# One encoder block on one core: each engine's instructions in the program's own order

## The chip, the cores and the metric

The kernel runs on one core of a Trainium2 chip. TensorE (PE) multiplies matrices and transposes, VectorE (DVE) and ScalarE (ACT) work elementwise, GpSimd (POOL) takes a little, SyncE (SP) issues the transfers. The time is that of one execution on the device in microseconds (us). The kernel before takes 1742.75 us, the median of three runs (1742.09 to 1745.59).

## The reference

256 tokens of 2048 channels, float32. What is computed, cut to its steps:

```python
mod = silu(c) @ w_cond + b_cond                  # six vectors: shift, scale, gate, twice
u = x * (1 + sc_m) + sh_m
cb, cc, ch, q, k, v, qi, ki, wi, ga, gb = split(u @ w_in)
y_a = cb * causal_dwconv3(cc * ch)               # short convolution
y_b = sparse_attention(q, k, v, qi, layer_norm(ki), wi)   # top 64 keys by an indexer's score
merged = sigmoid(ga) * (y_a @ w_a) + sigmoid(gb) * (y_b @ w_b)
x = layer_norm(ALPHA * x + (1 + g_m) * (merged @ w_o))    # the first norm
u = x * (1 + sc_f) + sh_f
a, b = split(u @ w_up)                           # 2 x 5632 channels
x = layer_norm(ALPHA * x + (1 + g_f) * ((gelu(causal_dwconv3(a)) * b) @ w_down))
```

## The kernel before

Every weight arrives as a *unit* of 1 MB (128 x 2048 float32), loaded by SP into one of four buffers `raw`. A unit is split for TensorE into an upper part, `hi` (ACT, line 82, a rounding copy), and the rest, `lo` (DVE, line 84, raw minus hi). There are three buffers of each. The activations are split in the same way, and a product is made of hi·hi, lo·hi and hi·lo. The function `unit` does load, hi and lo; a unit is multiplied by `xstat` (activations stationary, 24 matmuls of 512 columns), `wstat` (weights stationary, 16 matmuls of 512 columns and 16 of 256) or, in the segments, `seg_blocks`/`seg_tokens` (48 of 256 or 24 of 512).

The stages, in order: segments 0 to 3 of the input projection, beside which the 32 products of `c` with `w_cond` for the first shift and scale are made (`cond`, line 183: 1 MB and one DVE pass each, called a *dot* below) and u is made from them block by block (`modulated`); the index key `kw`; segment 4 with the indexer and the first two head groups of the attention; segments 5 and 6 with the other two and the convolution; 16 units `cb` of `w_in`; the gates and outputs (`columns`), each in units of `xstat`; `w_o` and the first norm; the first 24 of the 44 channel blocks of `w_up` and their part of `w_down`, then the other 20 and theirs; the second norm. A channel block takes two units, here slot *a* (product `ha`) and slot *g* (product `hg`). After slot a come: copy of one half of the product (ACT, line 119), sum (DVE, line 120), convolution (ACT line 333, DVE line 335 twice), gelu (ACT, line 653); after slot g: copy, sum, product (line 658), and the split of the result (ACT line 88, DVE line 89). Another 64 dots are spread over the stages by a running credit (`background`).

The order on every engine's queue is set by a scheduler, which goes by its own timing model. Where the program says `tc.issue_after`, an instruction stands behind another: that is so around the first norm (the last units of `w_o`, the first of `w_up`). The normalised rows are scaled and shifted by GpSimd (lines 618, 619) right behind that norm, while the first channel blocks run.

Of the kernel before, what the change touches and what calls it, by code (L numbers as in the profile page):

```python
# [41 lines left out]


C_B, C_C, C_H, C_Q, C_K, C_V, C_QI, C_KI, C_GA, C_GB = (
    0, 2048, 4096, 6144, 8192, 8704, 9216, 10240, 10320, 12368)


@with_exitstack
def hybrid_block(ctx: ExitStack, tc: tile.TileContext, t, out):
# [23 lines left out]
    def raw(src, width=D):  # L73
        r = wts.tile([P, D], F32, tag="raw", bufs=4, name="raw")
        nc.sync.dma_start(r[:, :width], src)
        return r

    def unit(src, width=D):

        r = raw(src, width)  # L80
# [28 lines left out]
    def wstat(pss, ws, x, m=P):  # L109

        for k in range(KB):
            for ps, (hi, lo) in zip(pss, ws):
                wh, wl = hi[:, k * m:(k + 1) * m], lo[:, k * m:(k + 1) * m]
                nc.tensor.matmul(ps, wh, x.both(k), start=k == 0, stop=k == KB - 1, skip_group_check=True)  # L114
                nc.tensor.matmul(ps[:, :S], wl, x.parts(k)[0], start=False, stop=k == KB - 1, skip_group_check=True)  # L115
# [6 lines left out]
    def xstat(ps, ws, x, b0, first, last, done=None):  # L122

        def tokens(n, units):
            s = slice(n * P, (n + 1) * P)
            for j in units:
                hi, lo = ws[j]  # L130
                for i in range(G4):
                    xh, xl = x.parts(b0 + j * G4 + i)
                    wh, wl = hi[:, i * 512:(i + 1) * 512], lo[:, i * 512:(i + 1) * 512]
                    a = first and j == 0 and i == 0
                    z = last and j == len(ws) - 1 and i == G4 - 1
                    nc.tensor.matmul(ps[n], xh[:, s], wh, start=a, stop=False)  # L136
                    nc.tensor.matmul(ps[n], xh[:, s], wl, start=False, stop=False)  # L137
                    end = nc.tensor.matmul(ps[n], xl[:, s], wh, start=False, stop=z)  # L138
            return end

        every = range(len(ws))
        end = tokens(0, every)
        if done:
            mid = done(0) or end
            with tc.issue_after(end.ins):
                tokens(1, every[:-1])
            with tc.issue_after(mid.ins):
                tokens(1, every[-1:])
            done(1)
        else:  # L150
            tokens(1, every)

    def groups(n, last):

        return [(g, 1) for g in range(n)] if not last else [(g, 1) for g in range(n - 3)] + [(n - 3, 3)]
# [9 lines left out]


# [6 lines left out]
    row_of(c_col, [c_b[:, g * 512:(g + 1) * 512] for g in range(4)])  # L173
    bcond = const.tile([P, 6, KB], F32)
    nc.sync.dma_start(bcond, t["b_cond"])
    mhalf = const.tile([P, 1], F32)
    nc.vector.memset(mhalf, -0.5)
    mod = const.tile([P, 6, KB], F32)


    def cond(p, k):
        r = raw(t["w_cond"][p * KB + k])
        nc.vector.scalar_tensor_tensor(  # L183
            r, r, 1.0, c_b, op0=ALU.mult, op1=ALU.mult, accum_out=mod[:, p, k:k + 1])
        one = 0.0 if p in (0, 3) else 1.0
        nc.vector.tensor_scalar(
            mod[:, p, k:k + 1], mod[:, p, k:k + 1], bcond[:, p, k:k + 1], one,
            op0=ALU.add, op1=ALU.add)

    later = [(p, k) for p in (2, 3, 4, 5) for k in range(KB)]  # L190
    credit = [0.0]

    def background(rate):
        credit[0] += rate
        while credit[0] >= 1.0 and later:
            credit[0] -= 1.0
            cond(*later.pop(0))
# [4 lines left out]

    def modulated(k):
        g, i = divmod(k, G4)
        cond(0, k)
        cond(1, k)
        if i == 0:
            xt[g] = act(f"xt{g}")
            nc.sync.dma_start(xt[g], t["x_t"][g])
        x, (hi, lo) = xt[g][:, i, :], u.parts(k)  # L210
        nc.scalar.activation(x, x, AF.Identity, scale=mod[:, 1, k:k + 1], bias=mod[:, 0, k:k + 1])
        nc.scalar.copy(hi, x)  # L212
        nc.gpsimd.tensor_sub(lo, x, hi.bitcast(F32))  # L213

    def proj(c0, name):
        ps = bank(name)
        wstat([ps], [unit(t["w_in"][c0])], u)
        return ps
# [4 lines left out]
    vt = acts.tile([P, NT, 512], F32, tag="act", bufs=25, name="v")  # L223
    cc, ch = [[acts.tile([P, NT, 512], F32, tag="act", bufs=25, name=f"{x}{g}") for g in range(4)] for x in ("cc", "ch")]
# [3 lines left out]

    def flat(x):
        return x.rearrange("p a b -> p (a b)")  # L230
# [21 lines left out]

    done = [0]

    def ahead(k):

        while done[0] < k:
            modulated(done[0])
            done[0] += 1
# [27 lines left out]
    def segment(sg, to, each=None, lead=0):  # L287

        k0, k1, u0, u1, n = SEGS[sg]
        num = (u1 - u0) * 512 // n  # L290
        start = max(done[0], k1)
        if lead:
            ws, pss = [], [[bank("s") for _ in range(n // 256)] for _ in range(lead)]
            for k in range(k0, k1):
                ahead(k + 1)
                if k - k0 < lead:
                    ws.append(unit(t[f"w_s{sg}"][k - k0], (k1 - k0) * n))
                for j in range(len(ws)):
                    for kk in range(k0 if j == k - k0 else k, k + 1):
                        for c in range(n // P):  # L300
                            seg_blocks(pss[j][c // 2][:, c % 2 * S:(c % 2 + 1) * S], ws[j], kk, kk - k0, n, c,
                                       kk == k0 and c % 2 == 0, kk == k1 - 1)
        ahead(k1)
        for j in range(num):
            if j < lead:
                ps = pss[j]
            else:
                w = unit(t[f"w_s{sg}"][j], (k1 - k0) * n)
                ps = [bank("s") for _ in range(n // 256)]
                seg_unit(sg, j, w, ps)  # L310
            seg_end(sg, j, ps)
# [4 lines left out]
    segment(0, 4, lead=2)  # L316
    segment(1, 5)
    segment(2, 8)

    conv_a = const.tile([P, KB, 3], F32)  # L320
    nc.sync.dma_start(conv_a, t["conv_a"])
    conv_f = const.tile([P, NFF, 3], F32)
    nc.sync.dma_start(conv_f, t["conv_f"])
    ln1 = const.tile([P, 2, KB], F32)
    nc.sync.dma_start(ln1, t["ln1_cols"])
    idx_gb = const.tile([P, 2, 2], F32)
    nc.vector.memset(idx_gb, 0.0)
    for j in range(2):
        nc.sync.dma_start(idx_gb[64 * j:64 * j + 64, j, :], t["idx_gb"])
# [17 lines left out]
    def indexer():  # L347

        zz = tmp.tile([P, 2, P], F32, tag="t1k", bufs=4, name="zz")
# [25 lines left out]

        for n in range(NT):
# [3 lines left out]
            for h0 in range(0, IH, per):  # L380
# [8 lines left out]
                for i in range(per):  # L389
# [377 lines left out]
```

## Time and profile before

| | |
|---|---|
| median of three runs | 1742.75 us |
| profiled execution | 1740.17 us, of it the span 1738.4 us |
| PE busy | 1691.0 us (97%), mean granted clock 0.989 |
| DVE busy | 1235.8 us (71%) |
| ACT busy | 759.3 us (44%) |
| POOL busy | 81.6 us (5%) |
| transfers | 419.58 MB, 241 GB/s over the span |

A share of the span is an average over stages, so the stages are looked at one by one. In a timeline a row gives the start, the duration, engine, line and operation; what stands in brackets is how long the engine was idle before, and who ended that. PE's ends are modelled, so a matmul's price is best taken as the distance between starts, or as stretches divided by their matmuls.

### The profile page before, as it was taken

To read this page: it belongs to the slowest core of one execution; us is meant where nothing else is said; L and a number is where in the kernel's file an instruction comes from. 1 tells how busy PE (TensorE), PEld (TensorE's weight loads), DVE (VectorE), ACT (ScalarE), POOL (GpSimd) and SP (SyncE) were. 2 spreads that over 40 slices of the span, in tenths; PEclk is the share of its full clock that TensorE was granted. 3 is DMA by queue.
4 is the path that set the end of the run, shared out by engine and by line. 5 is a ranking of instruction groups with operands and counts; after the bars stand their busy time and mean duration, and the time that the engine had idled before them with its cause. 6 is when DMAs were issued, how large, how long until landed. Compare 5 with 4: busy or idle time off the path is not lost.

```text
span 1738.4 us, 21791 instructions
## 1 busy us (share of the span) xinstructions
PE 1691.0 (97%) x8942; PEld 1451.3 (83%) x8942; DVE 1235.8 (71%) x1350; ACT 759.3 (44%) x824; POOL 81.6 (5%) x56
## 2 busy tenths in 40 slices
PE   6998999999999999999999799999999999999997
PEld 6888799988888888888888688888888888888885
DVE  6888968988888666776777797666654466666555
ACT  5553334444545333433333545544433344454431
POOL 1011100000000000000000530000000000000002
PEclk8999999999999999999999999999999999999999
DMA  8998865677786777777787476555555555555651
GB/s 329 342 363 345 334 244 202 238 258 269 272 309 242 273 288 267 265 280 272 266 302 282 143 290 218 194 186 185 187 192 194 193 194 184 181 193 188 233 194 64
DMA packets 63268, 419.58 MB, mean 241 GB/s; under 512 B 7616, under 2 KB 7744, under 8 KB 14528
## 3 DMA queue, kind: packets, MB, share of 16 engines
q1 hardware_dynamic: 63168, 418.18, 66.1%
q8 instruction: 70, 1.15, 0.2%
q14 instruction: 30, 0.25, 0.0%
HBM read 416.06 MB, written 2.10 MB: 241 GB/s over the span
## 4 chain that ended last, share of the span: by engine, by line
PE 89%; DVE 6%; DMA 2%; issue 1%; ACT 1%; POOL 0%; POOLq 0%; DVEq 0%; ACTq 0%
PE ha L114 9%; PE hg L114 9%; PE m L137 5%; PE m L136 5%; PE m L138 5%; PE ha L115 5%; PE hg L115 5%; PE y L138 5%; PE y L137 5%; PE y L136 5%; PE g L137 3%; PE g L136 3%; PE g L138 3%; PE s L250 3%; PE s L251 3%; PE s L249 3%
## 5 line engine op out<-in xcount | busy, mean ns | idle before, releaser
L84 DVE TENSOR_TENSOR lo<-raw,hi 128x2048 fp32r<-128x2048 f32 (+2 forms) x301 | 675.9, 2247 | 385.0 <-ACT hi L82 384.2
L82 ACT CAST hi<-raw 128x2048 fp32r<-128x2048 f32 (+2 forms) x301 | 561.0, 1864 | 662.5 <-PE m L138 150.0
L114 PE MATMUL ha<-u,hi 128*128 128x512 f32 x704 | 250.7, 397 | 0.0
L114 PE MATMUL hg<-u,hi 128*128 128x512 f32 x704 | 248.9, 395 | 0.0
L183 DVE SCALAR_TENSOR_TENSOR raw<-raw,c_b 128x2048 f32<-128x2048 f32 x96 | 223.1, 2328 | 35.8 <-DMA raw<-in_w_cond 29.4
L115 PE MATMUL ha<-u,lo 128*128 128x256 f32 x704 | 198.2, 281 | 4.3 <-DVE lo L84 4.3
L115 PE MATMUL hg<-u,lo 128*128 128x256 f32 x704 | 197.3, 280 | 0.0
L114 PEld LDWEIGHTS ha<-u,hi 128*128 128x128 f32 x704 | 132.7, 189 | 31.0 <-issue 0.2
L114 PEld LDWEIGHTS hg<-u,hi 128*128 128x128 f32 x704 | 131.9, 187 | 30.8
L237 PE MATMUL s<-u,hi 128*128 128x256 f32 x448 | 129.9, 293 | 9.7 <-ACT u L212 7.3
L115 PEld LDWEIGHTS ha<-u,lo 128*128 128x128 f32 x704 | 133.8, 190 | 4.7 <-DVE lo L84 4.6
L136 PE MATMUL y<-hi,h 128*128 128x512 f32 x352 | 137.0, 389 | 0.0
L137 PE MATMUL y<-lo,h 128*128 128x512 f32 x352 | 136.9, 389 | 0.0
L138 PE MATMUL y<-hi,h 128*128 128x512 f32 x352 | 136.9, 389 | 0.0
L115 PEld LDWEIGHTS hg<-u,lo 128*128 128x128 f32 x704 | 133.0, 189 | 0.0
L239 PE MATMUL s<-u,lo 128*128 128x256 f32 x448 | 127.6, 290 | 3.8 <-DVE lo L84 3.7
L238 PE MATMUL s<-u,hi 128*128 128x256 f32 x448 | 128.8, 289 | 0.7 <-POOL u L213 0.7
L250 PE MATMUL s<-lo,u 128*128 128x512 f32 (+1 forms) x304 | 116.1, 382 | 3.6 <-DVE lo L84 3.5
L251 PE MATMUL s<-hi,u 128*128 128x512 f32 (+1 forms) x304 | 116.5, 383 | 0.0
L249 PE MATMUL s<-hi,u 128*128 128x512 f32 (+1 forms) x304 | 113.6, 381 | 1.4 <-ACT hi L82 1.4
L137 PE MATMUL g<-lo,u 128*128 128x512 f32 x256 | 99.9, 390 | 0.0
L138 PE MATMUL g<-hi,u 128*128 128x512 f32 x256 | 99.8, 390 | 0.0
(172 smaller groups left out, 2643.9 us busy)
## 6 DMA issues: line engine op xcount, KB each, us to landing
raw<-in_w_cond SPq DMA_DIRECT2D x96, 1024.0 KB, 5.3
raw<-in_w_up SPq DMA_DIRECT2D x88, 1024.0 KB, 4.8
raw<-in_w_s SPq DMA_DIRECT2D x56, 1024.0 KB, 5.0
raw<-in_w_down SPq DMA_DIRECT2D x44, 1024.0 KB, 4.8
raw<-in_w_g SPq DMA_DIRECT2D x32, 1024.0 KB, 4.9
raw<-in_w_in SPq DMA_DIRECT2D x16, 1024.0 KB, 4.9
raw<-in_w_a SPq DMA_DIRECT2D x16, 1024.0 KB, 4.9
raw<-in_w_b SPq DMA_DIRECT2D x16, 1024.0 KB, 5.1
```

Of the source, the lines that this page charges most:

```text
L82: nc.scalar.copy(hi[:, :width], r[:, :width])
L84: nc.vector.tensor_sub(lo[:, :width], r[:, :width], hi[:, :width].bitcast(F32))
L114: nc.tensor.matmul(ps, wh, x.both(k), start=k == 0, stop=k == KB - 1, skip_group_check=True)
L115: nc.tensor.matmul(ps[:, :S], wl, x.parts(k)[0], start=False, stop=k == KB - 1, skip_group_check=True)
L136: nc.tensor.matmul(ps[n], xh[:, s], wh, start=a, stop=False)
L137: nc.tensor.matmul(ps[n], xh[:, s], wl, start=False, stop=False)
L138: end = nc.tensor.matmul(ps[n], xl[:, s], wh, start=False, stop=z)
L183: nc.vector.scalar_tensor_tensor(r, r, 1.0, c_b, op0=ALU.mult, op1=ALU.mult, accum_out=mod[:, p, k:k + 1])
L237: nc.tensor.matmul(ps, hi[:, a], xh, start=first, stop=False, skip_group_check=True)
L249: nc.tensor.matmul(ps[m], xh[:, s], hi[:, a], start=first and k == k0, stop=False)
L250: nc.tensor.matmul(ps[m], xh[:, s], lo[:, a], start=False, stop=False)
L251: nc.tensor.matmul(ps[m], xl[:, s], hi[:, a], start=False, stop=last and k == k1 - 1)
```

## The change

Everything is issued under `tc.manual_schedule()`: each engine's queue has the order in which the program emits. The program first writes a list, `stream`, of steps (one per unit), loads and single calls, and a loop at the end emits it. For each step s it emits `parts` of the step three further on (`AHEAD`), then one piece each of two queues of side work (attention, convolution), then at some steps a dot, then the products of s, then what follows s. There are four buffers of hi and of lo instead of three. The attention, the indexer and the convolution are generators that give way after each piece. The first norm is written out as `first_norm` and `first_norm2`: the token-0 half of the last `w_o` units goes first, rows are normalised by DVE and ACT, transposes are issued a group at a time, and the weights of the blocks behind it may not be split before it ends (`hold`). The rows' scale and shift on GpSimd come at channel blocks 6, 9, 12 and 15. Before the first product TensorE makes 40 transposes of the identity, and 20 more behind the first one (`keep_warm`). The second norm runs on DVE alone, and its last product is finished in halves of 256 columns.

```diff
+AHEAD = 3
+LOADS = 4
...
-        hi = wts.tile([P, D], F32R, tag="hi", bufs=3, name="hi")
-        nc.scalar.copy(hi[:, :width], r[:, :width])
-        lo = wts.tile([P, D], F32R, tag="lo", bufs=3, name="lo")
-        nc.vector.tensor_sub(lo[:, :width], r[:, :width], hi[:, :width].bitcast(F32))
-        return hi, lo
+        hi = wts.tile([P, D], F32R, tag="hi", bufs=4, name="hi")
+        nc.scalar.copy(hi[:, :n], r[:, :n])
...
+        lo = wts.tile([P, D], F32R, tag="lo", bufs=4, name="lo")
+        nc.vector.tensor_sub(lo[:, :n], r[:, :n], hi[:, :n].bitcast(F32))
...
+        def after_a():
+            x = t1k("ha")
+            total(x, pa[0])
+            y.append(t1k("hy"))
+            conv3(y[0], x, conv_f[:, f, :])
+            nc.scalar.activation(y[0], y[0], AF.Gelu_apprx_tanh)
...
+            if half == 0 and f in (6, 9, 12, 15):
+                do(ln_apply, (f - 6) // 3)
...
+    for s in stream:
...
+        at += 1
+        while prepared < min(at + AHEAD, len(steps)):
+            x = steps[prepared]
+            if x.hold and x.hold not in passed:
+                break
+            if not x.by_hand:
+                order.append(parts(x))
+            prepared += 1
+        order.append(lambda: [piece(x) for x in queues])
+        if later:
+            credit += s.cond
+            if credit >= 1.0:
+                credit -= 1.0
+                order.append(later_dot())
+        if s.mm:
+            order.append(lambda s=s: s.mm(s.w))
+        if s.after:
+            order.append(s.after)
...
+    with tc.manual_schedule():
```

ScalarE in the channel blocks of `w_up`, before (`hi` the split of a coming unit, `ha` and `b` the copies of a product's half, `hy` the convolution, line 333, and the gelu, line 653, `h` the split result):

```order
L82 CAST hi_8581<-raw_8579 128x2048
L119 COPY b_8478<-hg_8393 128x256
L653 ACTIVATE hy_8435<-hy_8435 128x256
L88 CAST h08_8482<-hy_8435 128x256
L82 CAST hi_8627<-raw_8625 128x2048
L119 COPY ha_8525<-ha_8485 128x256
L333 ACTIVATE hy_8528<-ha_8525,conv_f_1014 128x256
L82 CAST hi_8674<-raw_8672 128x2048
L119 COPY b_8571<-hg_8486 128x256
L653 ACTIVATE hy_8528<-hy_8528 128x256
L82 CAST hi_8720<-raw_8718 128x2048
```

The same engine and place now (line 120 is the split, 167 the copy, 422 the convolution, 880 the gelu, 136 the split result):

```order
L120 CAST hi_7857<-raw_7719 128x2048
L167 COPY b_7897<-hg_7864 128x256
L136 CAST h02_7901<-hy_7850 128x256
L120 CAST hi_7906<-raw_7808 128x2048
L167 COPY ha_7943<-ha_7910 128x256
L422 ACTIVATE hy_7946<-ha_7943,conv_f_85 128x256
L880 ACTIVATE hy_7946<-hy_7946 128x256
L120 CAST hi_7953<-raw_7855 128x2048
L167 COPY b_7990<-hg_7957 128x256
L136 CAST h02_7901<-hy_7946 128x256
L120 CAST hi_7998<-raw_7861 128x2048
```

Before, a split of a coming unit stood between the convolution and the gelu of a block; now gelu stands directly behind the convolution, and the next split behind the gelu.

VectorE there, before (`lo` the split of a coming unit, `ha` and `b` the sums, `hy` twice line 335 and once the product, `h` the split result):

```order
L84 TENSOR_TENSOR lo_8583<-raw_8579,hi_8581 128x2048
L120 TENSOR_TENSOR b_8478<-b_8478,hg_8393 128x256
L658 TENSOR_TENSOR hy_8435<-hy_8435,b_8478 128x256
L89 TENSOR_TENSOR h08_8482<-hy_8435,h08_8482 128x256
L84 TENSOR_TENSOR lo_8629<-raw_8625,hi_8627 128x2048
L120 TENSOR_TENSOR ha_8525<-ha_8525,ha_8485 128x256
L335 SCALAR_TENSOR_TENSOR hy_8528<-ha_8525,conv_f_1014,hy_8528 128x255
L335 SCALAR_TENSOR_TENSOR hy_8528<-ha_8525,conv_f_1014,hy_8528 128x254
```

And now (line 126 is `lo`, 244 a dot, 168 the sums, 424 the convolution):

```order
L126 TENSOR_TENSOR lo_7717<-raw_7614,hi_7715 128x2048
L244 SCALAR_TENSOR_TENSOR raw_7620,mod_82<-raw_7620,c_b_78 128x2048
L168 TENSOR_TENSOR ha_7755<-ha_7755,ha_7722 128x256
L424 SCALAR_TENSOR_TENSOR hy_7758<-ha_7755,conv_f_85,hy_7758 128x255
L424 SCALAR_TENSOR_TENSOR hy_7758<-ha_7755,conv_f_85,hy_7758 128x254
L126 TENSOR_TENSOR lo_7767<-raw_7667,hi_7765 128x2048
L168 TENSOR_TENSOR b_7802<-b_7802,hg_7769 128x256
L898 TENSOR_TENSOR hy_7758<-hy_7758,b_7802 128x256
L137 TENSOR_TENSOR h00_7710<-hy_7758,h00_7710 128x256
```

The rows of this engine keep their sequence; the dot now has a fixed place between a `lo` and the sum behind it, and the `lo` of a row belongs to the unit three further on.

VectorE in segment 3, before (`lo` line 84, dots line 183, what is added to a dot line 186, sums of the segment's products line 285):

```order
L84 TENSOR_TENSOR lo_1456<-raw_1452,hi_1454 128x2048
L84 TENSOR_TENSOR lo_1514<-raw_1510,hi_1512 128x2048
L183 SCALAR_TENSOR_TENSOR raw_1544,mod_107<-raw_1544,c_b_78 128x2048
L285 TENSOR_TENSOR q3_114<-q3_114,s_1458 128x512
L183 SCALAR_TENSOR_TENSOR raw_1548,mod_107<-raw_1548,c_b_78 128x2048
L186 TENSOR_SCALAR mod_107<-mod_107,bcond_103 128x1
L285 TENSOR_TENSOR q3_114<-q3_114,s_1459 128x512
L186 TENSOR_SCALAR mod_107<-mod_107,bcond_103 128x1
L84 TENSOR_TENSOR lo_1562<-raw_1558,hi_1560 128x2048
```

And now (`lo` line 126, sums line 354, dots line 244, line 289 the addition behind two dots):

```order
L126 TENSOR_TENSOR lo_1545<-raw_1473,hi_1543 128x2048
L354 TENSOR_TENSOR q3_95<-q3_95,s_1547 128x512
L354 TENSOR_TENSOR q3_95<-q3_95,s_1548 128x512
L126 TENSOR_TENSOR lo_1603<-raw_1531,hi_1601 128x2048
L354 TENSOR_TENSOR cc0_97<-cc0_97,s_1605 128x512
L354 TENSOR_TENSOR cc0_97<-cc0_97,s_1606 128x512
L244 SCALAR_TENSOR_TENSOR raw_1534,mod_82<-raw_1534,c_b_78 128x2048
L244 SCALAR_TENSOR_TENSOR raw_1541,mod_82<-raw_1541,c_b_78 128x2048
L289 TENSOR_TENSOR mod_82<-mod_82,bcond_79 128x2
L126 TENSOR_TENSOR lo_1650<-raw_1599,hi_1648 128x2048
```

Before, both sums of a unit could stand behind the dots and the `lo` ahead of them; now the dots stand behind both sums of the second unit, and the next `lo` behind the addition to the dots. On ScalarE two instructions that make u from that addition stand ahead of the next split:

```order
L120 CAST hi_1543<-raw_1473 128x2048
L120 CAST hi_1601<-raw_1531 128x2048
L290 ACTIVATE u12_1641<-xt3_1633,mod_82 128x256
L295 ACTIVATE xt3_1633<-xt3_1633,mod_82 128x256
L120 CAST hi_1648<-raw_1599 128x2048
L120 CAST hi_1682<-raw_1635 128x2048
```

So the split of the unit after next is behind those two, and they are behind the dots.

## Rows read from the trace of the kernel before

**Rows 1.** Windows: start:end, length, busy of PE, PEld, DVE, ACT, POOL, clock, DMA share, GB/s.

```profile
0.00:220.00 220.00, 198.03 (x1151) 174.46 (x1152) 186.27 (x190) 101.55 (x113) 29.99 (x22) 0.95 0.91 343
220.00:960.00 740.00, 739.35 (x3822) 630.78 (x3821) 565.48 (x647) 311.12 (x319) 1.11 (x2) 1.00 0.72 266
960.00:1040.00 80.00, 67.40 (x364) 57.35 (x363) 68.92 (x86) 41.05 (x61) 39.69 (x24) 0.94 0.61 212
```

**Rows 2.** Windows of two stretches of 40 us: columns, and channel blocks.

```profile
640.00:680.00 40.00, 40.00 (x178) 33.11 (x178) 24.43 (x18) 15.77 (x9) 0.00 (x0) 1.00 0.74 282
1080.00:1120.00 40.00, 40.00 (x232) 35.26 (x231) 26.12 (x30) 19.57 (x25) 0.00 (x0) 1.00 0.52 184
```

**Rows 3.** Timeline of ACT in a channel block of w_up.

```profile
1132.16 0.41 ACT L88 CAST h<-hy 128x256 fp32r<-128x256 f32 x1 [2.64 <-DVE hy L658]
1132.57 1.91 ACT L82 CAST hi<-raw 128x2048 fp32r<-128x2048 f32 x1
...
1137.17 0.51 ACT L333 ACTIVATE hy<-ha,conv_f 128x256 f32<-128x256 f32 x1 [2.43 <-DVE ha L120]
...
1140.19 0.42 ACT L653 ACTIVATE hy<-hy 128x256 f32<-128x256 f32 x1
```

**Rows 4.** Timeline of DVE in the same block.

```profile
1131.18 0.42 DVE L120 TENSOR_TENSOR b<-b,hg 128x256 f32<-128x256 f32 x1
1131.70 0.43 DVE L658 TENSOR_TENSOR hy<-hy,b 128x256 f32<-128x256 f32 x1
...
1134.51 2.29 DVE L84 TENSOR_TENSOR lo<-raw,hi 128x2048 fp32r<-128x2048 f32 x1 [1.49 <-ACT hi L82]
1136.72 0.42 DVE L120 TENSOR_TENSOR ha<-ha 128x256 f32<-128x256 f32 x1
1137.71 1.01 DVE L335 SCALAR_TENSOR_TENSOR hy<-ha,conv_f,hy 128x255 f32<-128x255 f32 x2 [0.58 <-ACT hy L333]
```

**Rows 5.** Timeline: first norm on DVE, PE, POOL, and w_down's first matmul.

```profile
963.78 0.69 DVE L595 TENSOR_TENSOR v<-gm,m 128x512 f32<-128x512 f32 x1 [3.92 <-PE m L138]
...
982.64 3.61 PE L566 MATMUL zT<-ident,v 128*128 128x128 f32 x16 [8.20 <-ACT v L562]
...
996.09 3.38 DVE L183 SCALAR_TENSOR_TENSOR raw<-raw,c_b 128x2048 f32<-128x2048 f32 x1
...
1000.56 16.07 POOL L619 TENSOR_TENSOR v<-v,lnrow 128x512 f32<-128x512 f32 x6
...
1260.42 0.48 PE L136 MATMUL y<-hi,h 128*128 128x512 f32 x1
```

**Rows 6.** Timeline of PE: start of segment 3, last matmul of kw.

```profile
116.49 0.28 PE L237 MATMUL s<-u,hi 128*128 128x256 f32 x1
...
220.16 0.28 PE L115 MATMUL kw<-u,lo 128*80 128x256 f32 x1
```

**Rows 7.** Timeline of DVE and ACT in segment 3.

```profile
139.09 2.29 DVE L183 SCALAR_TENSOR_TENSOR raw<-raw,c_b 128x2048 f32<-128x2048 f32 x1
141.29 0.69 DVE L285 TENSOR_TENSOR v<-v,s 128x512 f32<-128x512 f32 x1
...
145.07 0.60 ACT L211 ACTIVATE xt<-xt,mod 128x256 f32<-128x256 f32 x1 [1.25 <-DVE mod L186]
145.70 0.41 ACT L212 CAST u<-xt 128x256 fp32r<-128x256 f32 x1
```

**Rows 8.** Groups by form: side work of attention and convolution.

```profile
L420 DVE SCALAR_TENSOR_TENSOR lg<-lg,sc 128x512 f32<-128x512 f32 x12 | 8.0, 684 | 1.5 <-PE lg L417 1.5
L424 DVE TENSOR_REDUCE mx<-lg 128x4 f32<-128x1024 f32 x4 | 4.9, 1218 | 0.0
L431 DVE TENSOR_SCALAR lg<-lg,sm 128x128 f32<-128x128 f32 x16 | 3.5, 281 | 0.0
...
L427 ACT ACTIVATE lg<-lg,mx 128x256 f32<-128x256 f32 x16 | 7.9, 498 | 0.1
```

**Rows 9.** Timeline of the tail: POOL's last instruction.

```profile
1733.44 1.59 POOL L629 TENSOR_TENSOR v<-v,ln 128x512 f32<-128x512 f32 x1
```

More of the change, by code (lines that the diff above doesn't have):

```diff
@@ L120, in total, with xstat @@
         nc.vector.tensor_add(dst, dst, ps[:, :S])
[L122 to L155, printed above, removed]
+    def xstat(ps, w, x, b0, n, first=False, last=False, cols=512):
+        s = slice(n * P, (n + 1) * P)
+        hi, lo = w
+        for c in range(0, 512, cols):
+            y = ps[:, c:c + cols]
+            for i in range(G4):
+                xh, xl = x.parts(b0 + i)
+                o = i * 512 + c
+                wh, wl = hi[:, o:o + cols], lo[:, o:o + cols]
+                a, z = first and i == 0, last and i == G4 - 1
+                nc.tensor.matmul(y, xh[:, s], wh, start=a, stop=False, skip_group_check=True)
+                nc.tensor.matmul(y, xh[:, s], wl, start=False, stop=False, skip_group_check=True)
+                nc.tensor.matmul(y, xl[:, s], wh, start=False, stop=z, skip_group_check=True)
     def row_of(cols, dst):
@@ L164, in row_of, with flat, beside, piece @@
             nc.scalar.copy(dst[g], ps)
+    def flat(x):
+        return x.rearrange("p a b -> p (a b)")
+    queues = {"attend": [], "conv": []}
+    def beside(queue, work, *a):
+        do(lambda: queues[queue].append(work(*a)))
+    def piece(queue):
+        while queues[queue]:
+            try:
+                next(queues[queue][0])
+                return
+            except StopIteration:
+                queues[queue].pop(0)
+    def drain(queue):
+        while queues[queue]:
+            piece(queue)
     c_col = const.tile([P, KB], F32)
@@ L193, in background, with keep_warm @@
[L193 to L197, printed above, removed]
+    half_sums = const.tile([P, 2, 2], F32)
+    conv_a = const.tile([P, KB, 3], F32)
+    conv_f = const.tile([P, NFF, 3], F32)
+    ln1 = const.tile([P, 2, KB], F32)
+    idx_gb = const.tile([P, 2, 2], F32)
+    nc.vector.memset(idx_gb, 0.0)
+    def keep_warm(n):
+        ps = abank("warm")
+        for _ in range(n):
+            nc.tensor.transpose(ps[:, :P], ident, ident)
@@ new lines, in dot, with use @@
+    def dot(p, k, halves=False):
+        def use(r):
+            for h in range(2 if halves else 1):
+                a = slice(h * 1024, (h + 1) * 1024) if halves else slice(0, D)
+                nc.vector.scalar_tensor_tensor(
+                    r[:, a], r[:, a], 1.0, c_b[:, a], op0=ALU.mult, op1=ALU.mult,
+                    accum_out=half_sums[:, p, h:h + 1] if halves else mod[:, p, k:k + 1])
+            if p > 1 and k == KB - 1:
+                nc.vector.tensor_add(mod[:, p], mod[:, p], bcond[:, p])
+        return Load(t["w_cond"][p * KB + k], -D if halves else D, use)
@@ L210, in modulated @@
[L210 to L218, printed above, removed]
+        if k == 0:
+            stream.extend([dot(0, 0, True), dot(1, 0, True)])
+        else:
+            if i == 0:
+                do(xload, g)
+            stream.extend([dot(0, k), dot(1, k)])
@@ L285, in seg_end, with ahead, segment, mm @@
                 nc.vector.tensor_add(y, y, p)
-    def segment(sg, to, each=None, lead=0):
+    made = [0]
+    def ahead(k):
+        while made[0] < k:
+            modulated(made[0])
+            made[0] += 1
+    def segment(sg, to, first=0, each=None, cond=0.0):
         k0, k1, u0, u1, n = SEGS[sg]
         num = (u1 - u0) * 512 // n
[L291 to L302, printed above, removed]
-        ahead(k1)
[L304 to L309, printed above, removed]
+        start = max(made[0], k1)
+        ahead(k1)
+        for j in range(first, num):
+            ps = []
+            def mm(w, j=j, ps=ps):
+                ps += [bank("s") for _ in range(n // 256)]
                 seg_unit(sg, j, w, ps)
-            seg_end(sg, j, ps)
+            step(t[f"w_s{sg}"][j], mm, lambda j=j, ps=ps: seg_end(sg, j, ps), (k1 - k0) * n, cond)
             ahead(start + min(to - start, (to - start) * (j + 2) // num))
@@ L428, in attend, with weights @@
                                      accum_out=sm[:, i:i + 1])
+            return lg, sm
+        def weights(lg, sm):
             nc.vector.reciprocal(sm, sm)
@@ L498, in columns @@
+        step(t["w_in"][j], mm, after, cond=0.3)
+    do(drain, "conv")
+    do(drain, "attend")
     def columns(name, w, c, x, each):
[L500 removed]
+        ps = []
         for g in range(4):
[L502 to L512 removed]
@@ L514, in hybrid_block, with mm, gated, gate_row @@
-    ma = [gated(c, ya, 0, "w_a") for c in range(4)]
+            def mm(w, g=g):
+                if g == 0:
+                    ps.extend([bank(name), bank(name)])
+                for n in range(NT):
+                    xstat(ps[n], w, x, g * G4, n, g == 0, g == 3)
+            step(t[w][c * 4 + g], mm, (lambda: [each(n, ps[n]) for n in range(NT)]) if g == 3 else None, cond=0.6)
+    def gated(c, x, gate, w, m):
+        sg = []
+        def gate_row(n, ps):
+            if n == 0:
+                sg.append(rows_tile("sg"))
+                m.append(rows_tile("ma"))
+            nc.scalar.activation(sg[0][:, n, :], ps, AF.Sigmoid)
+        columns("g", "w_g", gate * 4 + c, u, gate_row)
+        columns("m", w, c, x, lambda n, ps: nc.vector.tensor_mul(m[-1][:, n, :], ps, sg[0][:, n, :]))
@@ L560, in modulated2, with gains, normed @@
+    def gains():
+        nc.vector.tensor_mul(ab[:, 0, :], ln1[:, 0, :], mod[:, 4, :])
+        nc.vector.tensor_mul(ab[:, 1, :], ln1[:, 1, :], mod[:, 4, :])
+        nc.vector.tensor_add(ab[:, 1, :], ab[:, 1, :], mod[:, 3, :])
+    do(gains)
+    po = pm
+    ends = [step(t["w_o"][12 + g]) for g in (1, 2, 3)]
+    def normed(n, rs, off, on_act):
         for g in range(KB // G4):
             y = v[g][:, n, :]
-            nc.scalar.activation(y, y, AF.Identity, scale=rs, bias=off)
-            ps = abank("zT")
@@ new lines, in parts2, with first_norm @@
+    def parts2(n, g, x, h, eng):
+        w = u2.pair(g * G4 + 2 * h)
+        hi, lo = w[:, :, 0, n * P:(n + 1) * P], w[:, :, 1, n * P:(n + 1) * P]
+        nc.scalar.copy(hi, x[:, 2 * h:2 * h + 2, :])
+        eng.tensor_sub(lo, x[:, 2 * h:2 * h + 2, :], hi.bitcast(F32))
+    up1 = Step(t["w_up"][NFF], None, None, D, 0.0, None, True)
+    def first_norm():
+        ws = [s.w for s in ends]
+        for n in (0,):
+            for i, w in enumerate(ws):
+                xstat(po[n], w, mg, (i + 1) * G4, n, False, i == 2)
+        gated_rows(3, 0, po[0])
+        mean, rs = moments(st, 0)
+        off0 = offset(mean, rs)
+        normed(0, rs, off0, ())
+        for i in (0, 1):
+            xstat(po[1], ws[i], mg, (i + 1) * G4, 1)
@@ L652, in hybrid_block @@
-            conv3(y, x, conv_f[:, f, :])
-            nc.scalar.activation(y, y, AF.Gelu_apprx_tanh)
-            if f > 0:
-                wstat([pg], [unit(t["w_up"][NFF + f])], u2)
-            b = t1k("b")
-            total(b, pg)
-            nc.vector.tensor_mul(y, y, b)
-            split(*h.parts(f - f0), y)
-            with tc.issue_after(ends[1][1].ins):
-                background(0.75)
-        if half == 0:
-            while later:
-                cond(*later.pop(0))
-            gf = tmp.tile([P, D], F32, tag="row", name="gf")
-            gf = [gf[:, g * 512:(g + 1) * 512] for g in range(4)]
-            row_of(mod[:, 5, :], gf)
@@ L691, in hybrid_block, with mm @@
-            for g, m in groups(ng, final):
-                ws = [unit(t["w_down"][c * (NFF // G4) + f0 // G4 + g + i]) for i in range(m)]
-                xstat(pm, ws, h, g * G4, g == 0, g + m == ng, done if m > 1 else None)
-            if not final:
-                done(0)
-                done(1)
+            for g in range(ng - 3 if final else ng):
+                def mm(w, g=g, pm=pm, h=h, ng=ng):
+                    if g == 0:
+                        pm += [bank("y0"), bank("y1")]
+                    for n in range(NT):
+                        xstat(pm[n], w, h, g * G4, n, g == 0, g == ng - 1)
+                step(t["w_down"][c * (NFF // G4) + f0 // G4 + g], mm,
+                     (lambda c=c, pm=pm, half=half: [down_rows(c, n, pm[n], half) for n in range(NT)])
+                     if g == ng - 1 else None)
@@ new lines, in hybrid_block, with finish @@
+            if final:
+                last = [step(t["w_down"][c * (NFF // G4) + f0 // G4 + g]) for g in range(ng - 3, ng)]
+                def finish(pm=pm, h=h, ng=ng):
+                    for n in range(NT):
+                        for i, s in enumerate(last):
+                            xstat(pm[n], s.w, h, (ng - 3 + i) * G4, n, False, i == 2, 256 if n and i == 2 else 512)
+                        if n == 0:
+                            down_rows(3, 0, pm[0], 1)
+                            output(0)
+                    down_rows(3, 1, pm[1], 1, 256)
+                    output(1)
+                do(finish)
```

580 lines of the change are left out of this document (377 added, 203 removed).

## The prediction

> **What bounds the kernel now.** I read the windows by stage first. TensorE is the bound nearly everywhere: 739.35 of 740 us busy from 220 to 960, and 40.00 of 40 in a stretch of the columns and in one of the channel blocks [rows 1, 2]. The other two places are the start (198.03 of 220, transfers at a share of 0.91) and the first norm (67.40 of 80, clock 0.94) [rows 1]. So what could be won is 22 + 12.6 us there and a few at the end; in the long stages there is nothing, but there the kernel can lose, if a helper engine is late. What decides is whether hi and lo of each unit still come in time when every queue is strictly in the program's order.
>
> TensorE's price of a unit: 178 matmuls of 512 columns in 40 us [rows 2] are 0.225 each, 24 are 5.4 us. In the channel blocks 116 pairs of one 512 and one 256 take 40 us, 0.345 a pair; 16 pairs are a unit, two units a block: 11.04 us, or 11.1 with the small gaps.
>
> **The channel blocks (44 of them).** Now the queues make a ring. On ScalarE the split hi of the next step stands behind gelu of this block; on VectorE the sum of a block stands behind lo of the unit three further on. Start to start, from the two timelines [rows 3, 4]:
> - slot a: hi to lo 1134.51 - 1132.57 = 1.94; lo to sum 1136.72 - 1134.51 = 2.21; sum to convolution on ACT 0.45; that to DVE's two passes 0.54; these to gelu 1.01 and some 0.03; gelu 0.42 to the next hi. Together 6.60.
> - slot g: hi to lo 1.94; lo to sum 2.21; sum to product 1131.70 - 1131.18 = 0.52; product to the split h on ACT 1132.16 - 1131.70 = 0.46; that to the next hi 0.41. Together 5.54.
>
> A round is 12.14 us against TensorE's 11.1; a dot in it adds 2.2 (139.09 to 141.29 [rows 7]). Before, a hi stood between convolution and gelu, so ScalarE did not wait for VectorE's passes with the next split behind it: gelu, whose input was there at 1138.72, started at 1140.19 [rows 3, 4]. The ring was open, and VectorE had 1.49 us to spare before a lo [rows 4]. The lead of three units (16.7 us, of which hi, lo and two sums take 5) pays for a dozen us; then TensorE waits for each lo.
>
> First half: from the end of token 0's last product, T0 = 963.7 [rows 5], `w_down` started at 1260.42 - 963.7 = T0 + 297 before, and its fourth unit three units later, T0 + 313. Now: no block's weights may be split before the norm ends on VectorE. Before, that was at 996.09, T0 + 32 [rows 5]; with the norm's subtractions no longer beside GpSimd's long stretch I put it at T0 + 27. Three lo's follow (6.6), so the first sum comes at T0 + 34. From there to the lo of the fifth block two rounds and a third, with one dot: 31, so T0 + 65. The lo of `w_down`'s third unit is 21 rounds and 13 dots later: 21 x 12.14 + 13 x 2.2 = 283.5, T0 + 348.5; it takes 2.2 and that unit's product 5.4: the fourth starts at T0 + 356. That is **+43**, with the norm's own gain in it: TensorE's 8.20 wait [rows 5] shrinks, since the transposes now go by groups (some -9). If a round came down to TensorE's own 11.1, the dots alone would remain: 29 less a lead of 12 and less 9, +8. With a hop of 0.1 more in each of eleven places a round is 13.2, and it is +65.
>
> GpSimd's 16 multiplications and additions of rows now lie beside four of these blocks. Beside such work the dot took 3.38 and not 2.29, and GpSimd 16.07 for six, 2.7 each [rows 5]; 16 x 2.7 = 43 us, in which VectorE, some two thirds busy, loses a third of its work's time: 9. Before, this lay in the norm's shadow in part. I take **+6** (0 to 14). The Trainium skill, "SBUF — State Buffer", section "Who interferes with whom", has VectorE with two inputs in SBUF and GpSimd exclude each other for a whole instruction; the rows show both stretched instead, so the measurement decides; by the page's rule, each of 16 instructions of some 1.5 us held against a lo, it would be up to 24 us.
>
> Second half: 20 rounds without dots against TensorE's, 20 x 1.0 = 20, of which the lead that `w_down` (units of `xstat`, with little side work) has given back covers some 12: **+7** (3 to 12).
>
> **The start.** From segment 3 on two steps make one round: VectorE has lo, two sums, lo, two sums, two dots; ScalarE then u and xt behind the dots; then hi. By rows: 2 x 2.21 + 4 x 0.69 + 2 x 2.2 + 0.41 + 0.60 + 1.94 = 14.5 [rows 4, 7]; 2 units of 48 matmuls of 256 columns or 24 of 512 are 11. Before, segment 3 and kw took from 116.5 to 220.2, of which some 5 us of kw's stretch were already segment 4's [rows 6]: 99 us. Eight rounds of 14.5 and the lead's use at either end make 118 to 123: +19 to +24; transfers (0.91 of the time [rows 1]) then have room. The same order in segments 0 to 2 costs some 5 more (dots ahead of the splits), keep_warm and the loading by halves give a little. **+29** (20 to 33).
>
> **Attention and convolution.** Their pieces stand ahead of the products in TensorE's queue and have no lead: a transpose waits for a piece of VectorE one slot before. The slot with a second set of logits is a chain of lo 2.21, reciprocal and four scalings 4 x 0.28 + 0.17, two maskings 2 x 0.68, maximum 1.22, four exponentials on ScalarE 4 x 0.5, hi to lo 1.94 = 10.0, against a unit of 5.4 [rows 4, 8]: 4.6 over, in four head groups 18. A convolution slot: copy or activation 0.5 and two passes 1.0, twice, two sums 1.4, hi to lo 1.94, lo 2.21: 8.5, 3.1 over, eight of them 25. Of these 43 the slots between, with 1.9 us to spare each, give back some 9: **+34** (10 to 45). Before, side work that was not ready did not hold up the queues [rows 1]. The pieces of `merged` are +1.
>
> **The tail** loses GpSimd's leg, which ended at 1735.0 [rows 9], against VectorE that then did three rows and now four: **-1**.
>
> Sum: 43 + 6 + 7 + 29 + 34 + 1 - 1 = 119. TensorE's clock was 0.95 and 0.94 where it had gaps and 1.00 where it had none [rows 1]; now it has gaps in a third of the time, but where it waits for a lo anyway a slower clock costs little: +3. On the profiled execution's 1740.2 this is 1862; that execution lies 2.6 below the median of the runs, so on the median's scale 1864, of which I take 1862.
>
> **The rivals.**
> (1) *The lead hides the rings.* Three units are 16.7 us, VectorE is 71% busy and ScalarE 44%, and a queue's order could matter little. Then only gains stay: 9 at the norm, 1 at the tail, some 5 at the start, 1742.75 - 15 = 1728. It decides if a round with hops costs under 11.1 us; the rows give 12.1 and the dots are certain work in the same ring. Chance 0.07.
> (2) *The rings bind only where dots or pieces are in them.* If hops overlap better than in a trace where nobody hurried, the blocks cost +8, the second half 0, GpSimd 3, the start 20, attention 10 to 18: some +45, 1790. For it speaks that the hops were measured with slack; against it that the durations alone, without any hop, are 1.91 + 2.29 + 0.42 + 0.51 + 1.01 + 0.42 for slot a and 1.91 + 2.29 + 0.42 + 0.43 + 0.41 for slot g, 12.0 [rows 3, 4]. Chance 0.17.
> (3) *The clock follows the gaps.* At the norm it fell, behind a wait of 8.20 us, to a mean of 0.94 over 80 us [rows 1, 5]. With waits of 1 to 3 us in each round TensorE could stand for stretches at the lower level, 1.2 GHz, where a round costs it 22 us and not 11: five per cent of 500 such us are 25 more, 1887. Chance 0.1.
> (4) No change within 0.2% (about what a measurement of this kernel tells apart): gains at the norm and the start happen to cancel a small loss. Chance 0.02.
>
> **How the numbers follow.** The forecast, 0.64, has its own range from the terms' ends, of which not all fall on one side: 1825 to 1895. With (2) on the low side and (3) on the high one the range is 1790 to 1900; beyond it stay (1), (4) and the outer parts of (2) and (3). Faster 0.07, same 0.02, slower 0.91.
>
> **What would show it.** In the channel blocks of the first half the rounds of TensorE stand 12.1 us apart, 14.4 with a dot, and each product's wait is ended by lo on DVE; ScalarE's idle time before hi is none, before gelu 1 us ended by DVE. In segment 3 two units take 14.5, and waits are ended by lo or by u on ACT. Transposes of attention wait for VectorE's scalings. The window of the columns stays at 40 of 40. Wrong would be a first half of blocks that ends within 300 us of T0, or TensorE busy over 97% from 240 to 530.

## The result: 1880.03 us, slower by 7.8%

The changed kernel takes 1880.03 us (1879.37 to 1881.91, four runs) against 1743.47 (the kernel before, now with a fourth run); the ratio is 1.0784, 95% interval 1.0765 to 1.0803. Its profiled execution has a span of 1880.1 at a mean clock of 0.966.

The windows of the changed kernel, cut where TensorE goes from stage to stage (columns as in [rows 1]), answer to [rows 1]:

```profile
131.20:250.20 119.00, 103.02 (x586) 89.75 (x585) 91.30 (x89) 41.29 (x37) 6.63 (x9) 0.94 0.82 304
250.20:490.20 240.00, 220.07 (x1335) 195.98 (x1333) 160.63 (x235) 90.64 (x120) 1.11 (x2) 0.95 0.44 156
490.20:607.70 117.50, 106.23 (x569) 90.12 (x570) 78.45 (x102) 49.50 (x77) 0.00 (x0) 0.94 0.51 180
607.70:1051.90 444.20, 443.68 (x1997) 367.38 (x1995) 321.43 (x266) 176.82 (x137) 2.68 (x5) 1.00 0.80 296
1051.90:1398.20 346.30, 292.30 (x1569) 248.02 (x1569) 223.34 (x257) 143.85 (x195) 31.40 (x20) 0.94 0.55 199
1398.20:1757.40 359.20, 358.93 (x1859) 305.92 (x1857) 197.65 (x189) 150.83 (x158) 0.00 (x0) 0.99 0.51 181
```

The columns and the second half are still TensorE's; the other stages have idle time on every engine, and in segments 4 to 6 transfers take 0.44 of the time (0.66 before). That fits a ring of waits, in which no engine is full. By TensorE's stage ends (in us; the last three columns are differences to before; 49 is the 43 and GpSimd's 6):

| stage | before | after | forecast | all moves (e8) |
|---|---|---|---|---|
| start to `kw` | 220.3 | +29.8 | +29 | +24.9 |
| segment 4 to `cb` (attention, convolution) | 310.8 | +46.8 | +34 | +28.2 |
| columns, `w_o` | 442.9 | +1.3 | +1 | -0.1 |
| first norm, first half of blocks | 286.4 | +59.9 | +49 | -0.9 |
| `w_down`, second half | 356.8 | +2.4 | +7 | +1.8 |
| last `w_down`, second norm | 121.2 | +1.5 | -1 | -0.3 |

Here the prediction misread a row. The kernel before ran 24 other matmuls beside `kw`, and the prediction took these, "some 5 us of kw's stretch", for segment 4's. They are the last unit of segment 3: VectorE adds them to `ch`, which segment 4 does not make, and from 220.28 to the columns TensorE has the same 1905 matmuls as the changed kernel (windows below).

```profile
215.14 0.69 DVE L285 TENSOR_TENSOR ch<-ch,s 128x512 f32<-128x512 f32 x1 [0.60 <-PE s L251]
```

So all of this time counts into the first stage here. Where expectations below say 42 lost between `kw` and the columns, it is 46.8 by this count.

VectorE in the channel blocks (start, duration, operation, idle before it and its releaser) answers to [rows 4]:

```profile
1199.83 2.29 DVE L126 TENSOR_TENSOR lo<-raw,hi 128x2048 fp32r<-128x2048 f32 x1 [1.38 <-ACT hi L120]
1202.04 0.41 DVE L168 TENSOR_TENSOR ha<-ha 128x256 f32<-128x256 f32 x1
1203.03 1.00 DVE L424 SCALAR_TENSOR_TENSOR hy<-ha,conv_f,hy 128x255 f32<-128x255 f32 x2 [0.58 <-ACT hy L422]
1206.38 2.29 DVE L126 TENSOR_TENSOR lo<-raw,hi 128x2048 fp32r<-128x2048 f32 x1 [2.35 <-ACT hi L120]
1208.59 2.28 DVE L244 SCALAR_TENSOR_TENSOR raw<-raw,c_b 128x2048 f32<-128x2048 f32 x1
...
1213.95 2.29 DVE L126 TENSOR_TENSOR lo<-raw,hi 128x2048 fp32r<-128x2048 f32 x1 [1.39 <-ACT hi L120]
```

And ScalarE, in the second half, where there are no dots, answers to [rows 3]:

```profile
1640.24 1.90 ACT L120 CAST hi<-raw 128x2048 fp32r<-128x2048 f32 x1
...
1644.83 0.51 ACT L422 ACTIVATE hy<-ha,conv_f 128x256 f32<-128x256 f32 x1 [2.42 <-DVE ha L168]
1646.47 0.42 ACT L880 ACTIVATE hy<-hy 128x256 f32<-128x256 f32 x1 [1.13 <-DVE hy L424]
1646.79 1.89 ACT L120 CAST hi<-raw 128x2048 fp32r<-128x2048 f32 x1
...
1652.14 1.90 ACT L120 CAST hi<-raw 128x2048 fp32r<-128x2048 f32 x1
```

A round is 14.12 with a dot and 11.90 without, against 14.3 and 12.14 forecast. Each engine waits for the other in turn (VectorE 1.4 and 2.35 for hi, ScalarE 2.42 and 1.13 for VectorE). In the first half this sets TensorE's pace too; in the second it does not: there TensorE is busy 358.93 of 359.20, while VectorE and ScalarE go on at 11.9 a round.

VectorE in segment 3, to [rows 7]: from one pair's lo to the next is 14.61 (forecast 14.5), with 3.10 idle behind the dots while ScalarE makes u and hi:

```profile
178.94 2.29 DVE L126 TENSOR_TENSOR lo<-raw,hi 128x2048 fp32r<-128x2048 f32 x1 [3.10 <-ACT hi L120]
...
187.95 2.29 DVE L244 SCALAR_TENSOR_TENSOR raw<-raw,c_b 128x2048 f32<-128x2048 f32 x1
...
193.55 2.29 DVE L126 TENSOR_TENSOR lo<-raw,hi 128x2048 fp32r<-128x2048 f32 x1 [3.10 <-ACT hi L120]
```

Two waits of TensorE, one in the attention, one ahead of `w_down`:

```profile
530.80 1.09 PE L542 MATMUL pT<-ident,lg 128*128 128x128 f32 x4 [5.81 <-DVE lg L535]
...
1397.46 1.12 PE L191 MATMUL row<-ident,mod 128*128 128x128 f32 x4 [13.38 <-ACT gf L192]
```

The first is the transposes of the attention, which have no lead. The second was not in the forecast: the rows of the second gate need ScalarE, and ScalarE was still a whole round behind with the last block.

### The profile page after: what moved, and what is told of

It reads as the page before. It is cut to its first block, busy times and chain, and to the rows that moved or that the text cites. A ratio compares the mean times of both kernels' runs of the same rounds, so it can differ in the third digit from the quotient of the medians.

```text
span 1880.1 us, 21849 instructions
## 1 busy us (share of the span) xinstructions
PE 1745.0 (93%) x9026; PEld 1487.3 (79%) x9026; DVE 1238.0 (66%) x1308; ACT 751.8 (40%) x818; POOL 48.9 (3%) x48
## 4 chain that ended last, share of the span: by engine, by line
PE 49%; DVE 29%; ACT 17%; issue 3%; DMA 2%; SPq 0%; POOL 0%; ACTq 0%; DVEq 0%
DVE lo L126 14%; ACT hi L120 11%; DVE raw L244 5%; PE m L182 4%; PE m L183 4%; PE m L181 4%; PE y L182 4%; PE y L183 4%; PE y L181 4%; PE g L181 3%; PE g L182 3%; PE g L183 3%; DVE hy L424 2%; PE cb L162 2%; PE s L315 2%
## 5 line engine op out<-in xcount | busy, mean ns | idle before, releaser
L162 PE MATMUL ha<-u,hi 128*128 128x512 f32 x704 | 258.6, 407 | 6.5 <-ACT hi L120 4.5
L244 DVE SCALAR_TENSOR_TENSOR raw<-raw,c_b 128x2048 f32<-128x2048 f32 (+1 forms) x98 | 219.8, 2253 | 10.3 <-DMA raw<-in_w_cond 10.0
L163 PE MATMUL ha<-u,lo 128*128 128x256 f32 x704 | 202.9, 288 | 15.3 <-DVE lo L126 15.2
L314 PE MATMUL s<-u,hi 128*128 128x256 f32 x448 | 133.1, 297 | 16.5 <-ACT u L290 6.5
L182 PE MATMUL y<-lo,h 128*128 128x512 f32 (+1 forms) x356 | 138.6, 389 | 1.3 <-DVE lo L126 1.3
L181 PE MATMUL y<-hi,h 128*128 128x512 f32 (+1 forms) x356 | 138.7, 390 | 0.0
L183 PE MATMUL y<-hi,h 128*128 128x512 f32 (+1 forms) x356 | 138.4, 389 | 0.0
L315 PE MATMUL s<-u,hi 128*128 128x256 f32 x448 | 131.7, 294 | 3.1 <-POOL u L296 3.1
L316 PE MATMUL s<-u,lo 128*128 128x256 f32 x448 | 131.7, 294 | 1.2 <-DVE lo L126 1.2
L326 PE MATMUL s<-hi,u 128*128 128x512 f32 (+1 forms) x304 | 122.6, 403 | 10.5 <-DVE ch L354 5.3
L328 PE MATMUL s<-hi,u 128*128 128x512 f32 (+1 forms) x304 | 119.6, 393 | 0.0
L314 PEld LDWEIGHTS s<-u,hi 128*128 128x128 f32 x448 | 90.9, 203 | 18.6 <-ACT u L290 7.2
```

The lines of the kernel that those rows point to most:

```text
L181: nc.tensor.matmul(y, xh[:, s], wh, start=a, stop=False, skip_group_check=True)
L182: nc.tensor.matmul(y, xh[:, s], wl, start=False, stop=False, skip_group_check=True)
L183: nc.tensor.matmul(y, xl[:, s], wh, start=False, stop=z, skip_group_check=True)
L244: nc.vector.scalar_tensor_tensor(r[:, a], r[:, a], 1.0, c_b[:, a], op0=ALU.mult, op1=ALU.mult, accum_out=half_sums[:, p, h:h + 1] if halve ...
L314: nc.tensor.matmul(ps, hi[:, a], xh, start=first, stop=False, skip_group_check=True)
L315: nc.tensor.matmul(ps, hi[:, a], xl, start=False, stop=False, skip_group_check=True)
```

## Experiments

Each is the changed kernel with one edit, unless said otherwise. What was expected stands ahead of the result.

**e1_scheduler**

```diff
-    with tc.manual_schedule():
+    if True:
```

> The changed program with its queues ordered by the scheduler again (manual_schedule taken away), all else as changed. If the fixed order is the cause: the rings open and the time is near before, 1725 to 1760. If the new pieces themselves cost it (the hold at the norm, attention cut in pieces, dots at other rates): 1800 or more.

1747.2 us, ratio to before 1.0033 (1.0021 to 1.0044). The order is the cause: 133 of 137 us go with it. The rest is the first norm (columns' end to `w_down` 5 longer than before), where TensorE waited 14.49 for the rows (before 8.20 [rows 5]): the scheduler does not keep the sequence laid out for it, but puts three splits and a dot among VectorE's steps of the norm (969.81 to 985.28 of this trace).

**e2_gelu**: gelu is called at the start of `mm_g`, so behind the next step's `parts`.

> Gelu of a block is issued behind the next split hi instead of ahead of it. Ring theory: slot a falls from 6.6 to about 5.0, a round without a dot from 11.9 to TensorE's 11.1, with a dot from 14.1 to 12.8: the first half is shorter by 24 x 0.8 to 24 x 1.36, 19 to 33, the time 1847 to 1861. Rival (VectorE's work and the clock are the loss, not gelu's place): 1876 to 1884.

1841.18 us, 39 less, more than expected: with the blocks (320 to 287 us) the wait before `w_down` shrank too, 13.38 to 8.91.

**e3_dots**

```diff
-step(t["w_up"][f], mm_a, after_a, cond=0.37,   # and the same for slot g; columns: cond=0.6
+step(t["w_up"][f], mm_a, after_a, cond=0.0,    # columns: cond=0.85
```

> The 14 dots of the channel blocks lie in the columns instead (credit 0.85 a unit there, 0 in the blocks). Ring theory: each was 2.2 in a ring that already set the pace, so 31 go, all rounds are 11.9, the time is 1845 to 1855, and the columns stay at TensorE's pace. Rival (transfers and VectorE in the columns have no room for 14 more MB): what the blocks win the columns lose, 1865 to 1885.

1850.33 us, 30 less; the columns took 447.5 where they had taken 444.3. A dot in a ring that sets the pace costs its whole 2.2; in the columns, where TensorE sets it, 14 more cost 3.

**e4_gate**: `do(second_gate)` behind the fourth unit of `w_down`.

> The transposes for the second gate's rows, at which TensorE waited 13.75 us before w_down, are issued behind the fourth unit of w_down. If that wait is one of its place in TensorE's queue: 13 less, 1865 to 1869. Rival (the split units of w_down are late by as much anyway): 1876 to 1882.

1867.0 us, 13 less. The wait was one of place.

**e5_pieces**: the line with `piece(x)` stands ahead of the loop over `prepared`.

> A step's pieces of attention and convolution are issued ahead of the split of the unit three further on, not behind it. If transposes wait because VectorE has a lo (2.2, and its wait for hi) ahead of a piece's work: the 42 lost between kw and the columns shrink by 12 to 35, 1845 to 1868. Rival (the pieces wait for each other and for ScalarE's exponentials, whatever stands ahead): within 4 of 1880.

1858.97 us, 21 less, some 17 of them between `kw` and the columns. Work without a lead (pieces) had stood behind work with three units of it (lo).

**e6_make**: `make` for k of 2 and more goes to a list that is emptied behind the next step's `parts`.

> The making of u from a pair of dots is issued behind the next step's split. Ring theory: a round of segment 3 falls from 14.6 to 11.5 to 12.2, 8 of them save 19 to 24, of which a few come back at the start's transfers: 1857 to 1866. Rival (transfers set this pace, 4 MB a round): 1876 to 1882.

1882.23 us: nothing won, at the edge of the rival's range. (The profiled execution was the fastest of the four, 1877.54, and in it `kw` ended 5 sooner than in the changed kernel; the others took 1882.1 to 1882.5.) ScalarE and then TensorE in this kernel:

```profile
189.46 0.60 ACT L291 ACTIVATE u<-xt,mod 128x256 fp32r<-128x256 f32 x1 [5.05 <-DVE mod L290]
190.09 0.60 ACT L296 ACTIVATE xt<-xt,mod 128x256 f32<-128x256 f32 x1
190.60 1.90 ACT L121 CAST hi<-raw 128x2048 fp32r<-128x2048 f32 x1
195.52 1.92 ACT L121 CAST hi<-raw 128x2048 fp32r<-128x2048 f32 x1 [3.02 <-DMA raw<-in_w_s]
```

```profile
244.00 0.71 PE L163 MATMUL kw<-u,hi 128*80 128x512 f32 x1 [6.58 <-POOL u L297]
```

The round fell only to 13.3: u now holds up the split of the pair's second unit instead of the first's, whose raw comes late. And `kw`, which needs every u, waits 6.58 for the last. What of it is the transfers and what the place of u is not settled.

**e7_rings**

```diff
-            nc.scalar.activation(y[0], y[0], AF.Gelu_apprx_tanh)
+            waiting.append(lambda: nc.scalar.activation(y[0], y[0], AF.Gelu_apprx_tanh))
...
-            split(*h.parts(f - f0), y[0])
+            waiting.append(lambda: split(*h.parts(f - f0), y[0]))
...
             prepared += 1
+        order.append(lambda: [f() for f in waiting] and waiting.clear())
```

> In the channel blocks both gelu and the split of the result are issued behind the next step's hi and lo. Ring theory: no work of a block stands ahead of the next split and waits for VectorE; a round is TensorE's 11.1 with a dot too (VectorE has 7.3 and a dot 2.2), the first half is shorter by 40 to 48, the wait before w_down shrinks from 13.75 to under 8: 1818 to 1834. Rival (gelu's place was all there was to win): 1838 to 1844.

1817.85 us, 62 less, the 13 of e4 among them. First matmul of the blocks to the last before the gate's: 1061 to 1335.9, 275 us, as before the change (274); then no wait:

```profile
1335.89 1.92 PE L192 MATMUL row<-ident,mod 128*128 128x128 f32 x16
1337.57 0.48 PE L182 MATMUL y<-hi,h 128*128 128x512 f32 x1
```

**e8_all**: e4, e5, e6, e7 and the split of `ya` behind the next `parts`.

> All of these at once: pieces ahead, u, gelu and the splits of ya and h behind the next split, the gate's transposes behind the fourth unit of w_down. If the losses are separate: 1880 less 20, 20, 57 and 4, some 1780 (1765 to 1800). If one loss hides another: 1800 to 1820.

1794.69 us, 85 less: e5 and e7 add up (83), the others add nothing. 53 over before remain, all ahead of the columns (table). Which waits make them up was not taken apart.

**e9_hybrid**: e8_all, with `manual_schedule` only from the gate's rows on; the scheduler orders what is ahead.

> The kernel with all the moves of e8_all, but the scheduler orders everything up to the columns and the program only what follows, from the gate's rows and the first norm on. If what e8_all still loses against before (53) lies in the fixed order of the first 600 us: 1738 to 1747, and TensorE ends the columns at 974 as before. If the hand-laid norm and blocks have a loss of their own: 1750 or more.

1744.45 us (12 runs), ratio 1.0018 (1.0008 to 1.0029): 0.2% over before. So 50 of the 53 lay in the fixed order of the first 600 us, and the hand-laid norm with open rings costs nothing and wins nothing that shows. No version beat the kernel before.

**e10_warm**: 16 transposes of the identity ahead of each group of transposes in the pieces.

> The changed kernel with 16 transposes of the identity ahead of each of 21 groups of transposes in attention and convolution, 37 us of TensorE work at 0.11 each, which fill waits. If the lower clock is a part of the 42 lost there: the clock of 250 to 608 rises from 0.95 to 0.98 or more and the time stays within 8 of 1880 although some 15 of this work fits in no wait. If only the waits count: 15 to 25 longer, 1895 to 1905, whatever the clock does.

1888.33 us, 8 more. The window from the first matmul of segment 4 to the first of the columns, in the changed kernel and in this one:

```profile
250.10:607.62 357.52, 326.32 (x1905) 286.12 (x1904) 239.01 (x336) 140.15 (x196) 1.11 (x2) 0.95 0.46 164
```

```profile
248.12:613.47 365.35, 352.91 (x2240) 316.16 (x2239) 239.10 (x336) 140.72 (x196) 1.11 (x2) 0.98 0.45 161
```

TensorE has 37 us more of work (an estimate, 336 transposes at 0.11) and is busy for 26.6 more, so the old work ran some 10 faster at the higher clock; idle time fell by 19. The clock thus is part of the loss there, and the waits the larger part. The time, 8.3 over, lies at the edge of the first expectation and below the second, so it is this sum that tells them apart, not the total.

## Why the prediction held, step by step

The sign and the cause were right: two rings, both found in the order alone and priced from rows of before, came out at 11.90 (12.14) and 14.12 (14.3) in the blocks and 14.61 (14.5) in segment 3, and e1 shows that the order is what costs. The sum was 18 short, and some of its terms fit for another reason than the one given. (The tail's -1 came as +1.5; what made it was not looked at.)

**The rivals.** The durations alone, 12.0, were the reason against rival (2), that hops overlap. They are no floor: the measured 11.90 is shorter. In the rows above gelu takes 0.42 at 1646.47, but the next hi starts 0.32 after it. What speaks against (2) is the measured rounds themselves. Rival (1), that the lead hides the order, is right for the second half. A round there is 11.91, not 12.14, and TensorE's own is 11.31, not 11.1 (its blocks start from 1530.88 to 1745.70, 19 rounds, as far apart as before). So 20 rounds lose 12, and three units of lead cover all of it. From the fourth unit of `w_down` on, the stage takes 340.7 and took 340.4; the 2.4 of the table lie ahead of that.

**The first half.** The walk held:

```profile
1041.92 0.69 DVE L718 TENSOR_TENSOR v<-gm,m 128x512 f32<-128x512 f32 x1 [3.61 <-PE m L183]
...
1077.14 0.41 DVE L168 TENSOR_TENSOR ha<-ha 128x256 f32<-128x256 f32 x1
...
1393.40 2.29 DVE L126 TENSOR_TENSOR lo<-raw,hi 128x2048 fp32r<-128x2048 f32 x1 [2.33 <-ACT hi L120]
```

```profile
1416.64 0.39 PE L181 MATMUL y<-hi,h 128*128 128x512 f32 x1
```

With T0 now at 1041.92 the first sum was due at T0 + 34 and came at T0 + 35.2; the lo of `w_down`'s third unit was due at T0 + 348.5, with GpSimd's +6 at 354.5, and came at T0 + 351.5. But "the fourth starts at T0 + 356" left out the gate's transposes in TensorE's queue: it started at T0 + 374.7. Of these 18.7, 3 are the lo's, 13.4 the wait for the gate's rows (e4 gives 13 back), and 2 the matmuls behind that wait, the first nine of which start 0.43 apart and not 0.23. The gain named at the norm hardly came: TensorE's wait of 8.20 is 7.01 now.

**Ahead of the columns.** Before (three lines) and after (two; the third is in e10), cut at segment 3's start, segment 4's start and the columns:

```profile
0.00:116.45 116.45, 100.14 (x568) 88.28 (x569) 92.64 (x94) 60.27 (x78) 15.04 (x14) 0.93 0.93 340
116.45:220.28 103.83, 98.17 (x585) 86.38 (x585) 93.64 (x97) 41.28 (x35) 14.95 (x8) 0.98 0.90 346
220.28:531.05 310.77, 310.12 (x1905) 275.01 (x1904) 262.64 (x381) 139.22 (x190) 1.11 (x2) 1.00 0.69 251
```

```profile
0.00:131.15 131.15, 110.95 (x628) 99.53 (x629) 89.15 (x91) 60.76 (x75) 5.09 (x12) 0.91 0.81 295
131.15:250.10 118.95, 102.97 (x586) 89.66 (x585) 91.35 (x89) 41.19 (x37) 6.63 (x9) 0.94 0.82 304
```

The start's +29 was met by luck, at 29.8. Segment 3 and `kw` take 119.0, as forecast, but before they took 103.8 and not 99 (the misread row), so the ring costs 15 there and not 19 to 24. Segments 0 to 2, put at some 5, cost 14.7: some 6.6 are the 60 transposes of `keep_warm` (an estimate, 0.11 each), 4 slower matmuls, 4 idle time.

The attention and convolution were 13 short, outside their own range. Idle time there grew by 30.6, near the 34; the same 1905 matmuls kept TensorE busy for 16.2 more, at a clock of 0.95 for 1.00. That is the term that was mis-sized: the clock, +3 for the whole kernel. The waits too were not where the sum had them (who waited, for what: us in total, times, the longest):

```profile
PE pT L542 <- DVE lg L535: 11.3, 4, 5.8
PE kwT L446 <- DVE st L451: 4.8, 1, 4.8
PE kiT L467 <- DVE kiT L468: 4.5, 1, 4.5
PE pz L600 <- DVE cc L592: 3.3, 1, 3.3
```

The scalings (`pT`) cost 11.3 (18 forecast), the convolution's transposes (`pz`) 6.0 in all (25, before what other slots give back), and the indexer's (`kwT`, `kiT`) 9.3, which the forecast had left out.

**GpSimd.** That the rows "show both stretched instead" of an exclusive hold between VectorE and GpSimd was a wrong reading. After the change the two meet one instruction at a time:

```profile
1228.08 2.29 DVE L126 TENSOR_TENSOR lo<-raw,hi 128x2048 fp32r<-128x2048 f32 x1 [1.38 <-ACT hi L120]
1228.36 3.16 POOL L849 TENSOR_TENSOR v<-v,lnrow 128x512 f32<-128x512 f32 x1 [40.30 <-DMA lnrow<-in_ln_g]
...
1231.28 1.94 DVE L424 SCALAR_TENSOR_TENSOR hy<-ha,conv_f,hy 128x255 f32<-128x255 f32 x2 [0.58 <-ACT hy L422]
1231.60 1.34 POOL L850 TENSOR_TENSOR v<-v,lnrow 128x512 f32<-128x512 f32 x1
```

A lo that began first keeps its 2.29, and the multiplication beside it takes 3.16 and not 1.3; the two passes take 1.94 and not 1.00 when GpSimd is in between. Where both have more to do, they alternate: GpSimd's addition waits for a lo, and the dot behind that lo for the addition.

```profile
1184.46 2.46 DVE L126 TENSOR_TENSOR lo<-raw,hi 128x2048 fp32r<-128x2048 f32 x1 [0.85 <-ACT hi L120]
1186.84 3.37 DVE L244 SCALAR_TENSOR_TENSOR raw<-raw,c_b 128x2048 f32<-128x2048 f32 x1
```

```profile
1184.85 3.22 POOL L850 TENSOR_TENSOR v<-v,lnrow 128x512 f32<-128x512 f32 x1
```

The dot's 3.37 is the 3.38 of [rows 5], so the stretch there reads as both in turn. This agrees with the Trainium skill ("SBUF — State Buffer", "Who interferes with whom"): the contention over the port pair that the two share is an exclusive lock, and issue order decides who blocks. Its worst case, 24, did not come: the four rounds that hold them take 12.69, 16.45, 15.08 and 15.14 where 11.90 or 14.12 is the rule, 5.1 in all. The +6 was near, though the way to it was wrong: luck.

## What to carry to other kernels

In a fixed order, write down for each pair of engines the ring that a round closes, with start-to-start times from the trace; if it is longer than the bound engine's round, a lead only pays once: here it covered the 20 rounds without dots, and not the 24 with 14 dots among them. Work that waits for another engine's fresh result should not stand ahead of work for later units: split first, then gelu and the split of the result (62 us here), and pieces without a lead ahead of units that have one (21 us). A busy share of 71% and 44% says nothing against a ring: both shares fell when it closed.

## Not expected of the hardware

With 9% of TensorE's time idle in waits of up to 6 us the clock over the attention was 0.95, and the same matmuls kept it busy for 326.3 us and not 310.1; filling those waits with 37 us of useless transposes cost 8 us in all and brought the clock to 0.98.
